# Recurrence gates as two 64-row products at once, one channel tile at a time, with the pooling sums as scans and the mixer's shift on ScalarE

## The chip, the core and the metric

The kernel is one launch on one core of a Trainium2 chip. The metric is the device time of that launch in microseconds (us), as the median of three runs. What can be told from no change is about 0.2%, some 2 us here.

Five engines matter. PE is TensorE: it loads a stationary operand ("LDWEIGHTS", shown as PEld) and streams a moving operand past it ("MATMUL"). DVE is VectorE and ACT is ScalarE; ACT loads a table ("ACT_TABLE_LOAD") when the family of functions changes. POOL is GpSimd, and SP starts transfers. Each engine works through its own queue strictly in order: an instruction that waits holds up everything behind it on that engine. Matrix products land in PSUM, from which DVE or ACT read them.

## The reference: what is computed

One layer of a decoder trunk, for 1024 tokens of width 1024, in fp32. The part that the change touches is the mixer:

```python
proj = rms_norm(h) @ w_in              # 1024 x 1536: u_pool, u_lru, u_gate
# four pooling groups of 128 channels, windows 2, 4, 8, 16
outs.append((c - c_lag) / count - ug)  # mean of the last w tokens, less the token
y_pool = (einsum('bsgc,gcd->bsgd', d, pool_w) + pool_b) * pool_scale
# recurrence: 512 channels in 8 heads of 64
xb = causal_depthwise_conv(u_lru)
r = sigmoid(einsum('bshi,hij->bshj', uh, gate_a_w) + gate_a_b)
i = sigmoid(einsum('bshi,hij->bshj', uh, gate_x_w) + gate_x_b)
a = exp(8 * r * log_sigmoid(lru_L)); b = sqrt(1 - a**2) * (i * xb)
h_t = a_t * h_(t-1) + b_t              # then multiplied by gelu(u_gate)
h = h + concat(y_pool, y_lru) @ w_out
```

Behind it come a squared-ReLU MLP of width 4096, a gated per-layer embedding and a final norm, which the change leaves alone.

## The kernel before, in words

**Tiling.** Everything stands channels by tokens: a tile is 128 channels on the partitions by 1024 tokens. Each fp32 operand x is held as a pair x_hi, x_lo in the matrix engine's fp32r format, and a product is three MATMULs, hi·hi, hi·lo and lo·hi (`mm`, L310 to L328; the instruction is on L320). A MATMUL has a 128 x 128 stationary block and a moving operand of 512 tokens, so one 128-channel block against 1024 tokens is six MATMULs. `split` (L149 to L156) makes a pair: ACT copies the high part (L152), DVE subtracts it to get the low part (L153). Weights come ahead of use through a list, `todo`: fetched as wi_raw, split to wi_hi and wi_lo, two buffers each, so the split of one projection's weights begins when the projection two before it has ended.

**The mixer.** `project(i)` (48 MATMULs into ps_i) makes one 128-channel tile of the input projection. Its order before is: conv of four channel tiles (results H[0] to H[3], split into the pairs B[4] to B[7], which the trace calls y), project(0), project(1), gates of tiles 0 and 1, project(2), project(3), gates of tiles 2 and 3, project(4), the pooling products of groups 0 and 1 (`pool_mix(0)`), project(5), project(6), `pool_mix(1)`, project(7), project(8). `lru_gates(pair)` multiplies a channel tile by two 128 x 128 blocks, for r and i, each holding two heads of 64 x 64 on its diagonal and zeros elsewhere; ACT takes the sigmoids straight from PSUM (L526), and DVE multiplies i by the conv's result (L527). `lru_scan` is Exp, Tanh, Square and Sqrt on ACT (L533 to L541) and a first-order scan on DVE (L544). `pool_windows` sums a window of w tokens by log2(w) shifted adds (L561) with a copy of the head each (L562), then scales and subtracts (L564 to L566) and splits. `pool_mix` multiplies a group by its 128 x 128 weights, and DVE adds the bias and scales (L578).

**What sets the order.** A list scheduler in the framework turns the written order into one queue for each engine, by what is free first; the order is fixed when the program is built. PSUM is handed out by `psum` (L130 to L135) in turns: an odd turn takes one tile of [128, 1024] from a pool of two ("pp", names such as ps_i_931), an even turn takes two tiles of [128, 512] from a pool of four ("pd", names such as ps_i_0_481 and ps_i_512_482). A tile that is asked for waits until the tile that held its place has been read. The projections' results are read by DVE (`normed`, L489), the gates' results by ACT.

```python
    def psum(name, one=False):
        turn.append(name)
        if one or len(turn) % 2 == 1:
            return [(slice(0, S), banks(name))]
        return [(hs, bank(f"{name}_{hs.start}")) for hs in HALVES]
```

Of the kernel before, what the change touches and what calls it, by code (L numbers as in the profile page):

```python
# [9 lines left out]
AF = mybir.ActivationFunctionType  # L10
ALU = mybir.AluOpType

P = 128
S = 1024
D = 1024
DFF = 4096
HALF = 512
# [11 lines left out]
NLRU = 4  # L29
NPOOL = 4  # L30
# [7 lines left out]
COLS = {}  # L38
# [11 lines left out]
def block_kernel(  # L50
# [16 lines left out]
    nc = tc.nc  # L67
# [9 lines left out]
    H = [h_all[:, i] for i in range(NT)]  # L77
# [47 lines left out]
    def hl(i):  # L125
        return small[i // 2][:, HALVES[i % 2]]
# [3 lines left out]
# [6 lines that stand above are left out]
# [4 lines left out]
    def col(name, i):  # L140
        c = COLS[name] + i
        return vecs[:, c : c + 1]
# [161 lines left out]

    def small_weights(name, raw):
        hi, lo = hl(2), hl(3)
        split(raw, hi, lo)
        return hi, lo
# [21 lines left out]
    def kblk(t, k):  # L330
        return t[:, k * P : (k + 1) * P]
# [78 lines left out]
    def tables():  # L410

        one = ones_f[:, :16]
        tc.keep_in_program_order(
            nc.vector.tensor_tensor_scan(recip_t, one, one, 0.0, ALU.mult, ALU.add)
        )
        nc.vector.reciprocal(recip_t, recip_t)


        tc.keep_in_program_order(nc.vector.memset(T[5], 0.0))
        rv = T[5].rearrange("p (n a t c) -> p n a t c", n=2, a=2, t=2)  # L420
        for pair in range(2):
            for a in range(2):
                for par in range(2):
                    r = slice(64 * par, 64 * par + 64)
                    nc.sync.dma_start(rv[r, pair, a, :, r], gates[pair, a, par])

# [34 lines left out]
    lv = vecs[:, c0 : c0 + NLRU]  # L461
    neg, e, s, s2, poly, cpos, cneg = (sp[:, i] for i in range(7))
    nc.vector.tensor_scalar_mul(neg, lv, -1.0)
# [12 lines left out]
    nc.vector.scalar_tensor_tensor(cpos, poly, 16.0, neg, ALU.mult, ALU.add)  # L476
    nc.vector.tensor_scalar_mul(cneg, cpos, -1.0)

    def project(i):
# [24 lines left out]
    LSETS = ((H[4], H[5], H[6]), (H[7], T[3], T[4]))  # L504

    gate_w, mix_w = {}, {}

    def ask_gates(pair):
        gate_w[pair] = small_weights(f"gw{pair}", T[5][:, pair * HALF : (pair + 1) * HALF])

    def ask_mix():
        raw = wp.tile([P, S], F32, tag="raw", name="pw_raw")[:, :HALF]
        nc.sync.dma_start(raw, pool_w)
        mix_w[0] = small_weights("pw", raw)

    def lru_gates(pair):

        hi, lo = gate_w[pair]
        for t in range(2):
            o = 2 * pair + t  # L520
            ct, rt, _ = LSETS[t]
            for a, (dst, b) in enumerate(((rt, "ga_b"), (ct, "gx_b"))):
                ps = psum(f"ps_g{a}{o}")
                mm(ps, kblk(hi, 2 * a + t), kblk(lo, 2 * a + t), *B[4 + o], True, True)
                for hs, part in ps:
                    nc.scalar.activation(dst[:, hs], part, AF.Sigmoid, bias=col(b, o))  # L526
            nc.vector.tensor_tensor(H[o], H[o], ct, ALU.mult)  # L527

# [24 lines left out]
    def pool_windows(g, ps):  # L553
        w = WINDOWS[g]
        u, *st = T[:3]
        if ps:
            normed(u, ps)
        cur, step, n = u, 1, 0
        while step < w:
            nxt = st[n % 2]  # L560
            nc.vector.tensor_tensor(nxt[:, step:], cur[:, step:], cur[:, : S - step], ALU.add)  # L561
            nc.vector.tensor_copy(nxt[:, :step], cur[:, :step])  # L562
            cur, step, n = nxt, 2 * step, n + 1
        nc.vector.tensor_tensor(cur[:, : w - 1], cur[:, : w - 1], recip_t[:, : w - 1], ALU.mult)  # L564
        nc.vector.tensor_tensor(cur[:, : w - 1], cur[:, : w - 1], u[:, : w - 1], ALU.subtract)
        nc.vector.scalar_tensor_tensor(  # L566
            cur[:, w - 1 :], cur[:, w - 1 :], 1.0 / w, u[:, w - 1 :], ALU.mult, ALU.subtract
        )
        split(cur, *B[g])

    def pool_mix(pair):
        whi, wlo = mix_w[0]
        for t in range(2):
            g = 2 * pair + t
            ps = psum(f"ps_p{g}")
            mm(ps, kblk(whi, g), kblk(wlo, g), *B[g], True, True)
            for hs, part in ps:
                nc.vector.tensor_scalar(  # L578
                    T[5][:, hs], part, col("pool_b", g), col("pool_s", g), ALU.add, ALU.mult
                )  # L580
            split(T[5], *B[g])

    conv(0, ps_l[0])
    conv(1, ps_l[1])
    ask_gates(0)
    conv(2, ps_l[2])
    conv(3, project(0))
    pool_windows(0, project(1))
    lru_gates(0)
    ask_gates(1)  # L590
    pool_windows(1, project(2))
    ps = project(3)
    normed(T[0], ps)
    lru_scan(0)
    lru_gates(1)
    ask_mix()
    pool_windows(2, None)
    ps = project(4)
    pool_mix(0)
    pool_windows(3, ps)  # L600
# [513 lines left out]
```

## Time and profile before

| | |
|---|---|
| Median of three runs | 977.63 us (977.19 to 978.01) |
| The profiled execution | 977.54 us, of which the span from first to last instruction is 975.5 us |
| Mean granted TensorE clock | 0.998 |
| PE busy | 964.8 us, 99% of the span |
| DVE busy | 757.0 us, 78% |
| ACT busy | 442.7 us, 45% |
| The mixer's projections, gates and pooling products on PE | from 40.77 us to 155.01 us |

The profile is of one execution; its times are counted from the first instruction. A line L153 is line 153 of the kernel; names are those of the program's tiles with the buffer numbers left out, so `y<-h` on L152 is the high part of one of the pairs B. "[4.06 <-DVE t L489]" behind a row says that the engine stood idle for 4.06 us before it, and that DVE's instruction on L489 ended the wait. Ends of MATMULs are modelled and overlap the next one's start; the distance between starts is what counts. On DVE and ACT, too, a row's duration overlaps the next one's start by about 0.1 us, so a queue's length is counted from start to start.

### The profile page before, as it was taken

Reading aid. Unit: us, or ns where it says so; the run is one execution under the profiler, and the core shown is the slowest. Engines: PE = TensorE matmul, PEld = TensorE weight load, DVE = VectorE, ACT = ScalarE, POOL = GpSimd, SP = SyncE. Lnnn points to the kernel's source line nnn. Section 1 sums busy time; section 2 is a strip of 40 time slices with the busy share of each in tenths; the row PEclk is TensorE's granted clock in tenths of the full one; section 3 lists DMA queues with packets and bytes.
Section 4 is the critical chain, followed back from the end, with each engine's and each line's share of the span. In section 5 each row is a group of like instructions: output and inputs, shape, how many; then the busy total and the mean of one; then the engine's idle time right before and its main releaser. Section 6 shows DMA issues by size and latency. Waiting matters only on the chain.

```text
span 975.5 us, 11507 instructions
## 1 busy us (share of the span) xinstructions
PE 964.8 (99%) x4472; PEld 805.2 (83%) x4472; DVE 757.0 (78%) x885; ACT 442.7 (45%) x528; POOL 99.1 (10%) x72
## 2 busy tenths in 40 slices
PE   9999999999999999999999999999999999999996
PEld 7888888888788888888888888888888888888996
DVE  7999995449887777677777899879775669784976
ACT  7377643336543343334333544444343337552534
POOL 0000000002523322332331000000000000000210
PEclk9999999999999999999999999999999999999999
DMA  6301243110245345434533897356532341031122
GB/s 231 105 23 33 87 151 107 45 43 30 82 152 201 119 140 177 159 119 160 196 119 137 307 368 254 110 194 202 174 118 90 108 151 44 3 127 44 44 87 87
DMA packets 46198, 125.04 MB, mean 128 GB/s; under 512 B 5312, under 2 KB 7360, under 8 KB 46144
## 3 DMA queue, kind: packets, MB, share of 16 engines
q1 hardware_dynamic: 46000, 124.27, 36.9%
q8 instruction: 35, 0.57, 0.2%
q14 instruction: 19, 0.16, 0.1%
q10 hardware_dynamic: 144, 0.04, 0.0%
HBM read 90.74 MB, written 33.55 MB: 127 GB/s over the span
## 4 chain that ended last, share of the span: by engine, by line
PE 95%; DVE 3%; ACT 1%; DMA 1%; issue 0%; SPq 0%; DVEq 0%
PE ps_P_u L320 31%; PE ps_P_d L320 31%; PE ps_i L320 10%; PE ps_o L320 9%; PE ps_e L320 8%; PE ps_l L320 3%; PE ps_g L320 1%; PE ps_j L320 1%; PE ps_p L320 1%; DVE h L968 1%; DMA h<-in_xT 1%; DVE a L153 1%; DVE a L156 0%; DVE t L984 0%; DVE wu_lo L153 0%
## 5 line engine op out<-in xcount | busy, mean ns | idle before, releaser
L320 PE MATMUL ps_P_d<-a,wd_P_hi 128*128 128x512 f32 x880 | 271.1, 389 | 0.0
L320 PEld LDWEIGHTS ps_P_d<-a,wd_P_hi 128*128 128x128 f32 x880 | 165.2, 188 | 34.4
L320 PE MATMUL ps_P_d<-a,wd_P_lo 128*128 128x512 f32 x440 | 171.3, 389 | 0.0
L320 PE MATMUL ps_P_u<-a,wu_hi 128*128 128x512 f32 x512 | 157.7, 389 | 0.0
L320 PE MATMUL ps_P_u<-y,wu_hi 128*128 128x512 f32 x384 | 118.1, 389 | 0.0
L320 PEld LDWEIGHTS ps_P_u<-a,wu_hi 128*128 128x128 f32 x512 | 96.1, 188 | 19.9
L659 DVE TENSOR_TENSOR t<-t,ps_P_u 128x512 f32<-128x512 f32 (+1 forms) x80 | 62.6, 784 | 47.9 <-PE ps_P_u L320 47.7
L320 PE MATMUL ps_P_u<-a,wu_lo 128*128 128x512 f32 x256 | 99.6, 389 | 0.0
L320 PEld LDWEIGHTS ps_P_d<-a,wd_P_lo 128*128 128x128 f32 x440 | 82.6, 188 | 17.4 <-DVE wd_P_lo L153 0.3
L320 PEld LDWEIGHTS ps_P_u<-y,wu_hi 128*128 128x128 f32 x384 | 72.1, 188 | 14.9
L320 PE MATMUL ps_i<-a,wi_hi 128*128 128x512 f32 x288 | 77.1, 389 | 0.0
L320 PE MATMUL ps_P_u<-y,wu_lo 128*128 128x512 f32 x192 | 74.8, 390 | 0.4 <-DVE wu_lo L153 0.4
L153 DVE TENSOR_TENSOR a<-wd,a 128x1024 fp32r<-128x1024 f32 x56 | 67.1, 1219 | 5.2 <-ACT a L152 4.1
L152 ACT ACTIVATE a<-wd 128x1024 fp32r<-128x1024 f32 x56 | 58.8, 1057 | 21.2 <-PE ps_P_d L320 10.2
L320 PE MATMUL ps_o<-y,wo_hi 128*128 128x512 f32 x256 | 68.4, 389 | 0.0
L320 PEld LDWEIGHTS ps_i<-a,wi_hi 128*128 128x128 f32 x288 | 54.1, 188 | 11.2
L152 ACT ACTIVATE wu_hi<-wu 128x1024 fp32r<-128x1024 f32 x24 | 25.5, 1062 | 78.3 <-PE ps_P_u L320 43.9
L152 ACT ACTIVATE wu_hi<-wu_raw 128x1024 fp32r<-128x1024 f32 (+1 forms) x25 | 25.3, 1011 | 78.2 <-PE ps_P_u L320 44.8
L320 PEld LDWEIGHTS ps_P_u<-a,wu_lo 128*128 128x128 f32 x256 | 48.0, 188 | 10.0
L320 PEld LDWEIGHTS ps_o<-y,wo_hi 128*128 128x128 f32 x256 | 48.0, 188 | 10.0
L152 ACT ACTIVATE wd_P_hi<-wd 128x1024 fp32r<-128x1024 f32 x24 | 25.4, 1060 | 58.2 <-PE ps_P_d L320 58.0
L153 POOL TENSOR_TENSOR wg_lo<-wg_raw,wg_hi 128x1024 fp32r<-128x1024 f32 x4 | 9.9, 2478 | 408.7 <-DVE h L953 382.1
(224 smaller groups left out, 1634.2 us busy)
## 6 DMA issues: line engine op xcount, KB each, us to landing
wd<-act SPq DMA_DIRECT2D x56, 512.0 KB, 5.6
act<-t SPq DMA_DIRECT2D x32, 512.0 KB, 4.3
wu_raw<-in_w_up SPq DMA_DIRECT2D x16, 512.0 KB, 3.7
wu<-in_w_up SPq DMA_DIRECT2D x16, 512.0 KB, 4.6
act<-wu SPq DMA_DIRECT2D x16, 512.0 KB, 4.5
wd<-in_w_down SPq DMA_DIRECT2D x16, 512.0 KB, 6.2
h<-in_xT SPq DMA_DIRECT2D x15, 512.0 KB, 4.3
wg_raw<-in_w_gate SPq DMA_DIRECT2D x12, 512.0 KB, 3.3
```

Source lines behind the costliest of these rows:

```text
L152: pin(nc.scalar.activation(hi, src, AF.Copy))
L153: pin((eng or nc.vector).tensor_tensor(lo, src, f32(hi), ALU.subtract))
L320: ins = nc.tensor.matmul(ps, w, z[:, hs], start=first and z is zhi and w is whi, stop=last and w is wlo, skip_group_check=more,)
L659: (eng or nc.vector).tensor_tensor(to, to if y is None else y, x, ALU.add)
L968: nc.vector.scalar_tensor_tensor(hv, hv, col("g_fin", o), rfin[:, hs], ALU.mult, ALU.mult)
```

## The change

**Gates.** The zero blocks go. For each channel tile, head 0 (channels 0 to 63) and head 1 (channels 64 to 127) each get a stationary block of 64 rows by 128 columns, that head's r and i weights side by side. The two heads are issued in turn, one on the upper 64 rows of the array and one on the lower 64, into two PSUM results, each of which holds r for one head and i for the same head on its two halves of partitions. So there are as many gate MATMULs as before, 48, each on 64 rows. The sigmoids are taken by halves of the partitions: six ACT instructions on 64 partitions for each channel tile in place of three on 128. The gates' weights come in one transfer of 256 KB, with neither the clearing of T[5] nor the eight smaller transfers, and are split once, into the slots hl(0) and hl(1); the mixer's weights take hl(2) and hl(3).

**Order.** `lru_gates` is called for one channel tile at a time: behind project(0), project(1), project(3) and project(4).

**Pooling.** For the windows 4, 8 and 16 the sums are a scan over the first w tokens and a scan over the rest that adds the token that enters and subtracts the one that leaves, in place of two, three and four adds with their copies. The window of 2 stays.

**Shift.** The mixer's bias and scale are one ACT instruction for each part (Identity with scale and the bias pool_bs = pool_b · pool_scale), in place of DVE's.

```diff
@@ -302,8 +302,8 @@
-    def small_weights(name, raw):
-        hi, lo = hl(2), hl(3)
+    def small_weights(raw, i):
+        hi, lo = hl(i), hl(i + 1)
         split(raw, hi, lo)
         return hi, lo
...
@@ -416,13 +416,7 @@
-        tc.keep_in_program_order(nc.vector.memset(T[5], 0.0))
-        rv = T[5].rearrange("p (n a t c) -> p n a t c", n=2, a=2, t=2)
-        for pair in range(2):
-            for a in range(2):
-                for par in range(2):
-                    r = slice(64 * par, 64 * par + 64)
-                    nc.sync.dma_start(rv[r, pair, a, :, r], gates[pair, a, par])
+        nc.sync.dma_start(T[5][:, FIRST], gates)
...
@@ -476,6 +470,9 @@
+    c_b, c_s = COLS["pool_b"], COLS["pool_s"]
+    nc.vector.tensor_tensor(pool_bs, vecs[:, c_b : c_b + NPOOL], vecs[:, c_s : c_s + NPOOL], ALU.mult)
+
...
@@ -503,28 +500,39 @@
+    HEADS = slice(0, 64), slice(64, P)
     gate_w, mix_w = {}, {}
 
-    def ask_gates(pair):
-        gate_w[pair] = small_weights(f"gw{pair}", T[5][:, pair * HALF : (pair + 1) * HALF])
+    def ask_gates():
+        gate_w[0] = small_weights(T[5][:, FIRST], 0)
 
     def ask_mix():
         raw = wp.tile([P, S], F32, tag="raw", name="pw_raw")[:, :HALF]
         nc.sync.dma_start(raw, pool_w)
-        mix_w[0] = small_weights("pw", raw)
-
-    def lru_gates(pair):
-
-        hi, lo = gate_w[pair]
-        for t in range(2):
-            o = 2 * pair + t
-            ct, rt, _ = LSETS[t]
-            for a, (dst, b) in enumerate(((rt, "ga_b"), (ct, "gx_b"))):
-                ps = psum(f"ps_g{a}{o}")
-                mm(ps, kblk(hi, 2 * a + t), kblk(lo, 2 * a + t), *B[4 + o], True, True)
-                for hs, part in ps:
-                    nc.scalar.activation(dst[:, hs], part, AF.Sigmoid, bias=col(b, o))
-            nc.vector.tensor_tensor(H[o], H[o], ct, ALU.mult)
+        mix_w[0] = small_weights(raw, 2)
+
+    def lru_gates(o):
+
+
+        hi, lo = gate_w[0]
+        ct, rt, _ = LSETS[o % 2]
+        zhi, zlo = B[4 + o]
+        ps = [psum(f"ps_g{h}{o}") for h in range(2)]
+        halves = [
+            [(hs.start + n, x[:, n : n + HALF]) for hs, x in parts for n in range(0, hs.stop - hs.start, HALF)]
+            for parts in ps
+        ]
+        for n, (w, z) in enumerate(((hi, zhi), (hi, zlo), (lo, zhi))):
+            for (at, x0), (_, x1) in zip(*halves):
+                for r, x in zip(HEADS, (x0, x1)):
+                    nc.tensor.matmul(
+                        x, w[r, o * P : (o + 1) * P], z[r, at : at + HALF], start=n == 0, stop=n == 2
+                    )
+        for dst, b, rows in ((rt, "ga_b", HEADS), (ct, "gx_b", HEADS[::-1])):
+            for h, r in enumerate(rows):
+                for hs, part in ps[h]:
+                    nc.scalar.activation(dst[HEADS[h], hs], part[r], AF.Sigmoid, bias=col(b, o)[r])
+        nc.vector.tensor_tensor(H[o], H[o], ct, ALU.mult)
 
     def lru_scan(pair):
         for t in range(2):
@@ -555,12 +563,16 @@
         u, *st = T[:3]
         if ps:
             normed(u, ps)
-        cur, step, n = u, 1, 0
-        while step < w:
-            nxt = st[n % 2]
-            nc.vector.tensor_tensor(nxt[:, step:], cur[:, step:], cur[:, : S - step], ALU.add)
-            nc.vector.tensor_copy(nxt[:, :step], cur[:, :step])
-            cur, step, n = nxt, 2 * step, n + 1
+        cur = st[g % 2]
+        if w == 2:
+            nc.vector.tensor_tensor(cur[:, 1:], u[:, 1:], u[:, : S - 1], ALU.add)
+            nc.vector.tensor_copy(cur[:, :1], u[:, :1])
+        else:
+
+            nc.vector.tensor_tensor_scan(cur[:, :w], ones_f[:, :w], u[:, :w], 0.0, ALU.mult, ALU.add)
+            nc.vector.tensor_tensor_scan(
+                cur[:, w:], u[:, w:], u[:, : S - w], cur[:, w - 1 : w], ALU.add, ALU.subtract
+            )
         nc.vector.tensor_tensor(cur[:, : w - 1], cur[:, : w - 1], recip_t[:, : w - 1], ALU.mult)
         nc.vector.tensor_tensor(cur[:, : w - 1], cur[:, : w - 1], u[:, : w - 1], ALU.subtract)
         nc.vector.scalar_tensor_tensor(
@@ -575,27 +587,28 @@
             ps = psum(f"ps_p{g}")
             mm(ps, kblk(whi, g), kblk(wlo, g), *B[g], True, True)
             for hs, part in ps:
-                nc.vector.tensor_scalar(
-                    T[5][:, hs], part, col("pool_b", g), col("pool_s", g), ALU.add, ALU.mult
+                nc.scalar.activation(
+                    T[5][:, hs], part, AF.Identity, bias=pool_bs[:, g : g + 1], scale=col("pool_s", g)
                 )
             split(T[5], *B[g])
 
     conv(0, ps_l[0])
     conv(1, ps_l[1])
-    ask_gates(0)
+    ask_gates()
     conv(2, ps_l[2])
     conv(3, project(0))
+    lru_gates(0)
     pool_windows(0, project(1))
-    lru_gates(0)
-    ask_gates(1)
+    lru_gates(1)
     pool_windows(1, project(2))
     ps = project(3)
     normed(T[0], ps)
     lru_scan(0)
-    lru_gates(1)
+    lru_gates(2)
     ask_mix()
     pool_windows(2, None)
     ps = project(4)
+    lru_gates(3)
     pool_mix(0)
     pool_windows(3, ps)
     gate_out(0, project(5))
@@ -1069,17 +1082,20 @@
...
+    gx_b = np.roll(cols(gate_x_b), 64, axis=0)
...
-    gates = np.stack([np.asarray(g)[0].reshape(2, 2, 2, 64, 64) for g in (gate_a_w, gate_x_w)])
-    gates = gates.transpose(1, 0, 3, 4, 2, 5)
+    ga, gx = (np.asarray(g)[0].reshape(NLRU, 2, 64, 64) for g in (gate_a_w, gate_x_w))
+    gates = np.stack([np.stack([ga[:, 0], gx[:, 0]], 2), np.stack([gx[:, 1], ga[:, 1]], 2)])
+    gates = gates.transpose(0, 2, 1, 3, 4)
```

Three places in the queues. The first is PE behind project(0), whose last MATMULs write ps_i_0 and ps_i_512. y_121 and y_122 are the pair B[4] that channel tile 0's gates read; before, project(1) follows at once:

```order
L320 MATMUL ps_i_0_488<-a,wi_hi 128x512
L320 MATMUL ps_i_512_489<-a,wi_hi 128x512
L320 MATMUL ps_i_0_488<-a,wi_lo 128x512
L320 MATMUL ps_i_512_489<-a,wi_lo 128x512
L320 MATMUL ps_i_552<-a,wi_hi 128x512 x4
L320 MATMUL ps_i_552<-a,wi_lo 128x512 x2
```

And in the changed program:

```order
L320 MATMUL ps_i_0_481<-a,wi_lo 128x512
L320 MATMUL ps_i_512_482<-a,wi_lo 128x512
L528 MATMUL ps_g_539<-y_121,hl_135 128x512
L528 MATMUL ps_g_0_540<-y_121,hl_135 128x512
L528 MATMUL ps_g_539<-y_121,hl_135 128x512
L528 MATMUL ps_g_512_541<-y_121,hl_135 128x512
L320 MATMUL ps_i_567<-a,wi_hi 128x512 x3
L528 MATMUL ps_g_539<-y_122,hl_135 128x512
L528 MATMUL ps_g_0_540<-y_122,hl_135 128x512
```

The twelve gate MATMULs of tile 0 now stand between project(0) and project(1), with three of project(1)'s (ps_i_567) between the first four and the last eight.

The second place is ACT around the window of 8, whose result is split as y_117. Before, all gates' sigmoids (L526) are over by then:

```order
L526 ACTIVATE t<-ps_g_512_808,vecs 128x512
L526 ACTIVATE h<-ps_g_817,vecs 128x1024
L152 ACTIVATE hl_136<-pw_raw 128x512
L533 ACT_TABLE_LOAD
L533 ACTIVATE h<-h,sp 128x1024
L533 ACTIVATE h<-t,sp 128x1024
L534 ACTIVATE h<-h,sp 128x1024
L535 ACTIVATE h<-h 128x1024
L152 ACTIVATE y_117<-t 128x1024
```

And in the changed program, where L534 is the sigmoid and L541 to L543 are Exp, Tanh and Square:

```order
L152 ACTIVATE y_117<-t 128x1024
L541 ACT_TABLE_LOAD
L541 ACTIVATE h<-h,sp 128x1024
L542 ACTIVATE h<-h,sp 128x1024
L543 ACTIVATE h<-h 128x1024
L152 ACTIVATE wi_hi<-wi_raw 128x1024
L534 ACT_TABLE_LOAD
L534 ACTIVATE t<-ps_g_0_873,vecs 64x512
L534 ACTIVATE t<-ps_g_872,vecs 64x1024
L534 ACTIVATE t<-ps_g_512_874,vecs 64x512
L534 ACTIVATE h<-ps_g_872,vecs 64x1024
```

The sigmoids of channel tile 3 (ps_g_872, 873, 874) now stand behind the split y_117. ps_g_872 is a "pp" tile; by the turns, the next two "pp" tiles are those of pooling group 0 and of project(5), so project(5) takes the place of ps_g_872 and begins no sooner than the last row above has read it. Before, project(5) took the place of ps_g_817, which the second row of the fence before had read.

The third place is DVE up to the window of 8's result. Before (L561 is an add, L562 a copy, L565 the last step, L527 the gates' product):

```order
L561 TENSOR_TENSOR t<-t 128x1023
L562 COPY t<-t 128x1
L153 TENSOR_TENSOR wi_lo<-wi_raw,wi_hi 128x1024
L527 TENSOR_TENSOR h<-h 128x1024
L561 TENSOR_TENSOR t<-t 128x1022
L527 TENSOR_TENSOR h<-h 128x1024
L153 TENSOR_TENSOR hl_136<-pw_raw,hl_136 128x512
L562 COPY t<-t 128x2
L561 TENSOR_TENSOR t<-t 128x1020
L562 COPY t<-t 128x4
L566 SCALAR_TENSOR_TENSOR t<-t 128x1017
L564 TENSOR_TENSOR t<-t,recip_t 128x7
```

And in the changed program (L572 and L573 are the two scans, L552 the recurrence's scan, L535 the gates' product):

```order
L572 SCALAR_TENSOR_TENSOR t<-ones,t 128x8
L153 TENSOR_TENSOR wi_lo<-wi_raw,wi_hi 128x1024
L552 SCALAR_TENSOR_TENSOR h<-h,t 128x1024
L573 SCALAR_TENSOR_TENSOR t<-t 128x1016
L576 TENSOR_TENSOR t<-t,recip_t 128x7
L578 SCALAR_TENSOR_TENSOR t<-t 128x1017
L577 TENSOR_TENSOR t<-t 128x7
L535 TENSOR_TENSOR h<-h 128x1024
```

Three adds and three copies became two scans, and both gate products that stood ahead of the window's result now stand behind it.

More of the change, by code (lines that the diff above doesn't have):

```diff
@@ L461, in block_kernel @@
     lv = vecs[:, c0 : c0 + NLRU]
-    neg, e, s, s2, poly, cpos, cneg = (sp[:, i] for i in range(7))
+    neg, e, s, s2, poly, cpos, cneg, pool_bs = (sp[:, i] for i in range(8))
     nc.vector.tensor_scalar_mul(neg, lv, -1.0)
@@ L1074 @@
             cols(norm_mix_g), cols(norm_mlp_g), cols(norm_ple_g), cols(norm_final_g), cols(pool_b),
-            cols(pool_scale), conv, cols(conv_b), cols(gate_a_b), cols(gate_x_b), cols(lru_L),
+            cols(pool_scale), conv, cols(conv_b), cols(gate_a_b), gx_b, cols(lru_L),
             cols(b_ple_gate),
@@ L1093 @@
         "pool_w": c(np.asarray(pool_w)[0].transpose(1, 0, 2)).reshape(P, NPOOL * P),
-        "gates": c(gates),
+        "gates": c(gates).reshape(P, NLRU * P),
         "w_out": tiles(np.asarray(w_out)[0]),
```

## The prediction

> **What bounds the kernel now.** First the page's busy times and its chain of waits, to see which engine sets the end:
>
> ```profile
> PE 964.8 (99%) x4472; PEld 805.2 (83%) x4472; DVE 757.0 (78%) x885; ACT 442.7 (45%) x528; POOL 99.1 (10%) x72
> PE 95%; DVE 3%; ACT 1%; DMA 1%; issue 0%; SPq 0%; DVEq 0%
> ```
>
> PE is busy for 99% of the span, so a microsecond that PE stands idle in the mixer is a microsecond on the end, and one taken out of PE's work is gained, if PE has nothing else to wait for. The chain through the mixer (start, length, group) shows what is there to gain:
>
> ```profile
> 40.77 21.76 PE ps_i L320 x96
> 62.53 4.08 PE ps_g L320 x18
> ...
> 66.83 1.36 PE ps_g L320 x6
> ...
> 89.73 5.44 PE ps_g L320 x24
> ...
> 108.77 21.76 PE ps_i L320 x96
> ```
>
> The pieces follow each other without a gap: 21.76 / 96 = 0.227 us for each MATMUL of 512 tokens, and 48 gate MATMULs are 10.88 us. The view of waits, PE's own, gives its longest:
>
> ```profile
> PE ps_l L432 <- DVE ones L338: 1.3, 1, 1.3
> PE n_ps L394 <- DVE t L1037: 0.6, 1, 0.6
> ```
>
> Neither is in the mixer. So a gain must come from the gate MATMULs, and a loss from a wait that isn't there now. Then I followed DVE's and ACT's queues in the timeline, since both are nearly full (DVE 7.50 of 7.50 us, then 17.81 of 19.00; ACT 7.47, then 14.44):
>
> ```profile
> 62.50:70.00 7.50, 7.50 (x35) 6.21 (x34) 7.50 (x9) 7.47 (x10) 0.00 (x0) 1.00 0.19 70
> 70.00:89.00 19.00, 19.00 (x86) 15.73 (x85) 17.81 (x24) 14.44 (x14) 0.00 (x0) 1.00 0.13 42
> ```
>
> **The gate products.** If the two heads' MATMULs run beside each other, a pair takes what one takes now, and 24 x 0.227 = 5.44 us leave PE's queue. The trace has no 64-row MATMUL. Its bounds: no overlap, gain 0; full overlap, 5.44 us. I take the second, because the queue can feed one load and MATMUL each 0.114 us (2.74 us for 24, from start to start):
>
> ```profile
> 949.22 2.90 PE L320 MATMUL ps_e<-a 128*128 128x256 f32 x24
> 951.96 0.87 PE L320 MATMUL ps_j<-proj,proj 128*128 128x256 f32 x6
> ```
>
> The order changes ten times between 64 and 128 rows. Each change costs between 0 and 0.35 us (a MATMUL of 389 ns and a load of 188 in sequence, less the 227 of a step); I take 0, as the sum hardly depends on it (below). The Trainium skill, "TensorEngine Tiling (Array Packing)", Key Properties, says that a change of tiling mode drains the engine; no run so far shows that, and by it the ten changes would take up to 3.5 us of the 5.44.
>
> **Tile 0's gates come early.** They stand right behind project(0). In ACT's timeline:
>
> ```profile
> 51.28 1.06 ACT L152 ACTIVATE wi_hi<-wi_raw 128x1024 fp32r<-128x1024 f32 x1 [5.01 <-issue]
> 52.24 2.00 ACT L152 ACTIVATE y<-h 128x1024 fp32r<-128x1024 f32 x2
> ...
> 62.11 1.06 ACT L152 ACTIVATE wi_hi<-wi_raw 128x1024 fp32r<-128x1024 f32 x1 [0.36 <-PE ps_i L320]
> ```
>
> The wi_hi split at 51.28 waits for the end of project(0), and the first y stands behind it: its first half ends at about 53.25. PE, done with project(0) at 51.65 (40.77 + 10.88), waits some 1.6 us for y_121. DVE's y_122 comes 1.2 later (a subtraction like the adds below), and seven MATMULs ahead of it cover 1.1 of that. So project(1) ends at 51.65 + 1.8 + 1.4 (six pairs) + 10.9, about 65.7, where it was 62.5.
>
> **ACT late, DVE late.** ACT's next wi_hi waits for that end. From there its queue, with starts from these rows:
>
> ```profile
> 91.69 2.27 ACT L526 ACTIVATE h<-ps_g,vecs 128x512 f32<-128x512 f32 x3
> 93.84 1.28 ACT L526 ACTIVATE t<-ps_g,vecs 128x512 f32<-128x512 f32 x2
> 95.25 1.12 ACT L526 ACTIVATE h<-ps_g,vecs 128x1024 f32<-128x1024 f32 x1
> 100.67 1.16 ACT L533 ACTIVATE h<-t,sp 128x1024 f32<-128x1024 f32 x1 [1.11 <-DVE h L527]
> 101.73 1.13 ACT L534 ACTIVATE h<-h,sp 128x1024 f32<-128x1024 f32 x1
> 104.14 1.06 ACT L152 ACTIVATE y<-t 128x1024 fp32r<-128x1024 f32 x1 [0.32 <-DVE t L565]
> 105.10 1.14 ACT L534 ACTIVATE t<-t,sp 128x1024 f32<-128x1024 f32 x1
> 106.14 1.05 ACT L535 ACTIVATE t<-h 128x1024 f32<-128x1024 f32 x1
> 107.20 1.28 ACT L541 ACT_TABLE_LOAD   x1
> 108.50 1.06 ACT L541 ACTIVATE h<-h 128x1024 f32<-128x1024 f32 x1
> ```
>
> Start to start: a split 0.96, a table 1.30, Exp 1.06, Tanh 1.04, Square 1.06, a sigmoid of 1024 tokens 1.02, of 512 0.57 ((2.15 - 1.02) / 2). I give 64 partitions the time of 128, for the row counts tokens; half of it would be the lower bound. Wi_hi, table, Exp, y, table, three sigmoids, y_113, three sigmoids, Tanh and Square are 13.0 us: 65.7 becomes 78.7. Square frees DVE's L545 (L537 before). Before, that instruction stood ahead of DVE's restart at 78.66; now it is that restart.
>
> **The window of 8 on DVE.** Before, its result is there at 103.94 + 0.17 = 104.11:
>
> ```profile
> 78.66 1.29 DVE L489 TENSOR_TENSOR t<-ps_i,rstd 128x512 f32<-128x512 f32 x2 [1.19 <-PE ps_i L320]
> 92.64 2.28 DVE L544 TENSOR_TENSOR_SCAN h<-h,t 128x1024 f32<-128x1024 f32 x1
> 94.83 1.20 DVE L561 TENSOR_TENSOR t<-t 128x1023 f32<-128x1023 f32 x1
> 95.95 0.14 DVE L562 COPY t<-t 128x1 f32<-128x1 f32 x1
> 97.14 1.22 DVE L527 TENSOR_TENSOR h<-h 128x1024 f32<-128x1024 f32 x1
> 98.28 1.22 DVE L561 TENSOR_TENSOR t<-t 128x1022 f32<-128x1022 f32 x1
> 103.94 0.17 DVE L565 TENSOR_TENSOR t<-t 128x7 f32<-128x7 f32 x1
> ```
>
> From 78.7 on the queue loses five adds (1.13 each, 5.65), five copies (0.54) and both L527 (1.14 each, 2.28), and gains two long scans (2.20, as the recurrence's scan), two short ones (0.1) and L545 (1.14): 104.11 - 8.47 + 5.74 = 101.4. Bounds for a long scan: 1.13 as the adds, 2.20 as L544; I take 2.20, the same instruction on the same engine. The window of 16 behind it changes nothing for PE.
>
> **The new wait.** project(5)'s result goes to the place of ps_g_872, whose last sigmoid stands on ACT behind y_117, and y_117 waits for 101.4. From there: split 0.96, table 1.30, Exp 1.06, Tanh 1.04, Square 1.06, wi_hi 0.96, table 1.30, sigmoids 0.57, 1.02, 0.57 and the fourth to its end 1.12: 10.96 us, so project(5) starts at 112.4, where it started at 108.77: **+3.6 us**. PE would get there at 108.77 - 5.44 + 1.8 = 105.1 (up to 1 us later, for DVE reads ps_i4 behind y_118), so it stands idle for about 6 us, and the 5.44 us gained go into that. That is why overlap and mode changes hardly count. They enter only through project(1)'s end: without overlap 1.4 us later.
>
> Behind the wait, ACT has 5.7 us of shifts more and DVE that much less:
>
> ```profile
> L578 DVE TENSOR_SCALAR t<-ps_p,vecs x6: 798/802/1334, 109.0 to 142.5; 128x512 f32<-128x512 f32 x4, 128x1024 f32<-128x1024 f32 x2
> 109.00:133.00 24.00, 24.00 (x107) 19.87 (x107) 23.97 (x29) 8.94 (x9) 0.00 (x0) 1.00 0.23 81
> ```
>
> ACT has 15 of 24 us free there and DVE none, so this costs nothing and eases DVE; without that room it would be 5.7 us. The one transfer for eight and the memset lie before 40 us, beside PE's first products: 0.
>
> **The clock after the wait.** PE's only longer rest is the program's start, and there MATMULs come slowly:
>
> ```profile
> 1.31 4.64 PE L432 MATMUL ps_l<-ones 128*128 128x512 f32 x10 [1.31 <-DVE ones L338]
> 5.74 0.83 PE L320 MATMUL ps_l<-a,wl_hi 128*128 128x512 f32 x2
> ```
>
> Ten take 4.43 us, 0.443 each, where 2.27 would do: 2.2 us lost (the page's clock row doesn't show it). No wait of 6 us inside the program is in the trace. Bounds 0 and 2.2; I take 2.2, the start being the only rest of such length. The Trainium skill, "TensorE: Matmul & The Clock Gate", Part 1, has the array at half rate after an idle window of about 3.4 us until it has been busy for as long; the start agrees (4.43 us), and by its figure I estimate 1.7 us.
>
> **Sum.** 977.54 + 3.6 + 2.2 = 983.3 us; the profiled execution is 0.1 below the median, which I leave out.
>
> **Rivals.**
> (a) The wait without the slow clock: 977.5 + 3.6 = 981.1. For it: the clock row never shows a drop. Against: the start.
> (b) The gain arrives. If ACT reaches ps_g_872's fourth sigmoid before PE needs the place at 105.1, PE alone decides: 977.5 - 5.4 + 1.8, 973.9, and up to 3.5 more with mode changes. This asks for a result of the window of 8 at 94.5, 7 us sooner than worked out. Scans at the adds' rate give 2.1 of it, sigmoids at half their time another 2 to 4; all must come together.
> (c) Both cancel in part: scans at the adds' rate alone put project(5) at 110.3, so 979.1, or 981.3 with the slow clock; with sigmoids faster too, about 977.5.
> (d) Pairs that don't overlap: project(1) ends 1.4 us later, and with mode changes 0.5 more; 984.7 to 985.2.
>
> **How the numbers follow.** Forecast (wait and slow clock) 0.52; (a) 0.24; (b) 0.07; (c) 0.09; (d) 0.08. The likeliest one's own range is 982 to 984.6. The range for all, 978.8 to 985.2, leaves out (b) and parts of (c) and (d). A measurement of this kernel tells 0.2%, about 2 us, from no change: below 975.7 is faster, 0.06; between, 0.10 (the rest of (b), most of (c)); slower 0.84.
>
> **What would show it.** In the changed profile: a PE wait of about 2 us ahead of the first ps_g, on ACT's y; ps_g MATMULs in pairs 0.23 us apart; the L573 scans at 2.2 us; y_117 at about 101.4 and ACT's sigmoids of 64x512 at 0.69; a PE wait of about 6 us ahead of a ps_i, on ACT's L534, with that ps_i at 112.4; the ten or so MATMULs behind it 0.44 us apart; from there on all as before, later by 5.8. The forecast is wrong if PE's wait there is under 2 us, if it is on another engine, or if the end moves by something behind 115 us.

## The result, and the profile after

The changed kernel takes **985.34 us** (median of four runs, 984.95 to 986.67), the kernel before 977.78 us beside it: a ratio of 1.0081, 95% interval 1.0063 to 1.0098. It is slower by 7.6 us. The forecast was 983.3 us with a range up to 985.2: the sign and the mechanism came as told, the size was 2 us too small, and the time lies just outside the range. The term that failed is the +3.6 us by which project(5) was to start late; it measured 5.78 us. The profiled execution took 984.95 us, with a span of 983.2 us.

PE's waits in the changed kernel (engine and line, what it waited for, total, times, longest):

```profile
PE ps_i L320 <- ACT h L534: 6.6, 1, 6.6
PE ps_g L528 <- ACT y L152: 1.7, 1, 1.7
```

Neither stood in the profile of before, and both were forecast: the second is tile 0's gates behind project(0), the first is project(5), which waits for a sigmoid. PE's timeline around them:

```profile
102.83 1.66 PE L528 MATMUL ps_g<-y,hl 64*128 64x512 f32 x12
104.42 3.53 PE L320 MATMUL ps_p<-y,hl 128*128 128x512 f32 x12
114.55 2.07 PE L320 MATMUL ps_i<-a,wi_hi 128*128 128x512 f32 x4 [6.60 <-ACT h L534]
...
117.28 1.75 PE L320 MATMUL ps_i<-a,wi_hi 128*128 128x512 f32 x4
```

Tile 3's gates and the pooling products of groups 0 and 1 (ps_p) end at 107.95; then PE rests until 114.55. The first six MATMULs behind the rest take 2.73 us from start to start (114.55 to 117.28), where six times 0.227 are 1.36. The view of windows has the granted clock in the column ahead of the last two (102 to 114.5 us, then 114.5 to 119):

```profile
102.00:114.50 12.50, 5.85 (x28) 3.54 (x27) 9.48 (x13) 11.41 (x11) 0.00 (x0) 0.90 0.12 42
114.50:119.00 4.50, 4.45 (x11) 3.53 (x12) 3.20 (x3) 4.43 (x6) 0.00 (x0) 0.53 0.35 120
```

The chain of waits gives both parts their size. Before, project(5) and project(6) started at 108.77 and their 96 MATMULs took 21.76 us:

```profile
113.39 1.12 ACT h L534
114.55 23.96 PE ps_i L320 x96
...
163.00 17.23 PE ps_o L320 x76
```

The start is 5.78 us later, the 96 MATMULs take 2.20 us more, and from there on every piece has its old length: the output projection starts at 163.00 instead of 155.01. That is the whole loss: 7.99 us there, 7.7 us in the spans (983.2 and 975.5).

### The profile page after: what moved, and what is told of

Same layout as the page of the kernel before. It is cut to its first block, busy times and chain, and to the rows that moved or that the text cites. A ratio compares the mean times of both kernels' runs of the same rounds, so it can differ in the third digit from the quotient of the medians.

```text
span 983.2 us, 11513 instructions
## 1 busy us (share of the span) xinstructions
PE 964.2 (98%) x4472; PEld 801.4 (82%) x4472; DVE 747.3 (76%) x866; ACT 465.2 (47%) x551; POOL 99.1 (10%) x72
## 4 chain that ended last, share of the span: by engine, by line
PE 89%; DVE 5%; ACT 3%; issue 2%; DMA 1%; SPq 0%; DVEq 0%
PE ps_P_d L320 31%; PE ps_P_u L320 30%; PE ps_o L320 9%; PE ps_e L320 8%; PE ps_i L320 6%; PE ps_l L320 3%; PE ps_j L320 1%; DMA h<-in_xT 1%; DVE h L981 1%; ACT t L534 0%; DVE h L552 0%; ACT y L152 0%; DVE wu_lo L153 0%; ACT h L534 0%; DVE a L153 0%
## 5 line engine op out<-in xcount | busy, mean ns | idle before, releaser
L320 PE MATMUL ps_i<-a,wi_hi 128*128 128x512 f32 x288 | 79.3, 397 | 6.6 <-ACT h L534 6.6
```

The costliest lines, as they stand in the source:

```text
L320: ins = nc.tensor.matmul(ps, w, z[:, hs], start=first and z is zhi and w is whi, stop=last and w is wlo, skip_group_check=more,)
```

## The experiments

Each is an edit to the changed kernel, unless it says otherwise. The starts of all pieces shift by up to a microsecond from one execution to the next (project(0) starts at 40.8 us before, at 39.7 in the first run below), so distances are compared, not starts alone.

### The order on ACT alone

```diff
+                    sig = nc.scalar.activation(dst[HEADS[h], hs], part[r], AF.Sigmoid, bias=col(b, o)[r])
...
+        return sig.ins        # lru_gates: tile's last sigmoid
...
-    lru_gates(3)
+    last = lru_gates(3)
...
-    lru_scan(1)
+    with tc.issue_after(last):
+        lru_scan(1)
```

> The changed kernel with one order added: ACT's Exp, Tanh, Square and Sqrt of lru_scan(1) stand behind the last sigmoid of channel tile 3. Theory (project(5) waits for ps_g_872 because these stand ahead of its sigmoids): the sigmoids follow y_117's split at about 104.0 with no table load between, the fourth ends at about 108.1, PE is through with the pooling products at 107.95, so project(5) starts at about 108.2 instead of 114.55, and with no rest there is no slow clock either: 985.3 - 6.3 - 2.2 = 976.8 us (976 to 978). Rival (another wait, on DVE's reading of ps_i4 or on the pooling results, would hold PE anyway): 981 or more, with a PE wait on DVE of over 3 us.

Measured: 976.92 us, ratio to before 1.0002 (0.9993 to 1.0011). ACT's timeline, and PE's behind it:

```profile
101.82 1.06 ACT L152 ACTIVATE y<-t 128x1024 fp32r<-128x1024 f32 x1 [5.66 <-DVE t L578]
102.79 1.04 ACT L152 ACTIVATE wi_hi<-wi_raw 128x1024 fp32r<-128x1024 f32 x1
103.86 2.53 ACT L534 ACTIVATE t<-ps_g,vecs 64x512 f32<-64x512 f32 x3
106.41 2.39 ACT L534 ACTIVATE h<-ps_g,vecs 64x1024 f32<-64x1024 f32 x3
```

```profile
107.57 1.20 PE L320 MATMUL ps_i<-a,wi_hi 128*128 128x512 f32 x4 [0.77 <-ACT h L534]
```

Exp, Tanh, Square and two table loads no longer stand between y_117 (the first row) and the sigmoids, and DVE's part of the scan stands later with them; but for table loads the work is the same. The wait falls from 6.60 to 0.77 us, the slow clock is gone, and so is the whole loss. The cause is the place that project(5) gets in PSUM together with ACT's order. It is no gain over before yet: what the gates save goes into the wait of 1.69 us for y_121, these 0.77 us, and a gap of some 0.5 us between the two pooling products (their twelve MATMULs take 3.54 us with the border ahead of them, 2.88 before).

### The rest and the slow clock

```diff
-            mm(ps, kblk(whi, g), kblk(wlo, g), *B[g], True, True)
+            for _ in range(5 if g == 1 else 1):
+                mm(ps, kblk(whi, g), kblk(wlo, g), *B[g], True, True)
```

> The changed kernel with the second pooling product of pool_mix(0) computed five times over into the same PSUM tile: 24 MATMULs more, 5.4 us, in the place where PE rested for 6.6 us. Theory (the slow MATMULs behind the wait come from the rest): project(5) still starts at about 114.5, the rest before it is about 1.2 us, its MATMULs are 0.227 us apart from the first on, and 985.3 becomes 983.1 us (982.6 to 983.7). Rival (they are slow for another reason, the change of product or the reading of PSUM by ACT): still 0.44 us apart, 985.3 us.

Measured: 983.34 us, ratio 1.0067 (1.0052 to 1.0082), with PE's rows

```profile
103.85 9.01 PE L320 MATMUL ps_p<-y,hl 128*128 128x512 f32 x36
114.02 1.20 PE L320 MATMUL ps_i<-a,wi_hi 128*128 128x512 f32 x4 [1.16 <-ACT h L534]
```

24 MATMULs more, and the kernel is no slower: 6.5 us above its before, where the changed kernel was 7.6 above (the intervals of the two ratios overlap). The rows say more. Project(5) starts as late as ever (73.7 us behind project(0) in both), but its first four MATMULs take 1.20 us instead of 2.07, and by the chain its and project(6)'s 96 take 22.08 instead of 23.96. So the slow MATMULs come from the rest; filling it gets 1.9 of their 2.2 us back in the profiled execution. The other 0.3 us are there at a full clock too: the late scan above has 22.05 for the same 96, behind its 0.77 us.

### 128-row gates in the new places

```diff
+    def lru_gates(o):      # before's products and sigmoids, one tile at a time
+        pair, t = divmod(o, 2)
+        hi, lo = gate_w[pair]
...
+        for a, (dst, b) in enumerate(((rt, "ga_b"), (ct, "gx_b"))):
+            ps = psum(f"ps_g{a}{o}")
+            mm(ps, kblk(hi, 2 * a + t), kblk(lo, 2 * a + t), *B[4 + o], True, True)
```

> The changed kernel with the gate products as before (128 x 128 blocks with zeros, three sigmoids on 128 partitions a tile), in the new places, with the new pooling and the shift on ACT. Theory (the places make the wait, the halved sigmoids lengthen it): PE's gate work is back to 10.9 us, so it reaches project(5) at about 110.5; ACT is shorter by three sigmoids a tile; project(5) starts at about 112, after a rest of 1 to 2 us that is too short for the slow clock: 977.7 + 3.3 = 981.0 us (980 to 982.5). Rival (the 64-row form itself costs the time): 977 to 978 us.

Measured: 980.34 us, ratio 1.0039 (1.0024 to 1.0053); project(5) starts at 112.00 behind this wait:

```profile
PE ps_i L320 <- ACT t L527: 1.3, 1, 1.3
```

So 3.5 of the 7.6 us are lost without any 64-row product: this part belongs to the places. Project(5) starts 71.3 us behind project(0); in the changed kernel it was 73.7, before 68.0. What the 64-row form adds is on ACT: here project(5)'s place is free behind one sigmoid on 128 partitions (110.83 to 111.94), there behind the fourth on 64 (110.88 to 114.51). And as PE comes later and the place is free sooner, the rest is short and the clock stays full.

### Tile 3's gates beside tile 2's

```diff
     lru_gates(2)
+    lru_gates(3)
     ask_mix()
     pool_windows(2, None)
     ps = project(4)
-    lru_gates(3)
```

> The changed kernel with the gates of tile 3 right behind those of tile 2, both behind project(3) as before the change. Theory: project(5) no longer finds tile 3's gates in its place, so the wait of 6.6 us and the slow clock go; in exchange tile 3's products wait up to 3 us for PSUM, which DVE (project(3)'s result) and ACT (tile 2's sigmoids) must first read. 978.7 us (977.5 to 980.5). Rival (the wait only moves in full): 983 or more.

Measured: 980.33 us, ratio 1.0041 (1.0026 to 1.0056), 1.6 us above what was expected. Project(5) no longer waits; the wait for PSUM has moved to tile 3's gates, as told, and 2.85 us of it were enough to slow the clock, which I hadn't reckoned with:

```profile
94.42 1.65 PE L528 MATMUL ps_g<-y,hl 64*128 64x512 f32 x11 [2.85 <-DVE t L486]
```

```profile
96.00:104.00 8.00, 8.00 (x29) 6.46 (x29) 8.00 (x8) 7.04 (x9) 0.00 (x0) 0.79 0.19 66
96.07 12.70 PE ps_i L320 x48
```

Project(4) takes 12.70 us (the second line is from the chain), in the changed kernel 11.10 from the end of tile 2's gates to tile 3's (91.73 to 102.83): 1.6 us, the whole of what was not expected.

### The pooling products moved

```diff
     lru_gates(3)
-    pool_mix(0)
     pool_windows(3, ps)
     gate_out(0, project(5))
     lru_scan(1)
+    pool_mix(0)
     gate_out(1, project(6))
-    pool_mix(1)
     gate_out(2, project(7))
+    pool_mix(1)
     gate_out(3, project(8))
```

> The changed kernel with the pooling products moved only: groups 0 and 1 behind project(5), groups 2 and 3 behind project(7). By the turns of PSUM project(5) then takes the place of channel tile 2's gates, whose sigmoids ended at 97.3. Theory (the loss is the place that project(5) gets, and the rest and the slow clock that follow): the wait of 6.6 us and the slow clock go, PE's wait of 1.7 us for y_121 stays, and four times twelve gate MATMULs in about 1.6 us save 10.9 - 6.5 = 4.4 us: 977.6 + 1.7 - 4.4 = 974.9 us (974 to 976.5). Rival (the wait moves to the pooling products, which now take tile 3's place): 979 us or more.

Measured: 976.60 us, ratio 0.9993 (0.9983 to 1.0002). The large wait is gone and none has taken its place. But 1.7 us of the expected gain are missing. In the profiled execution, where nothing at all is gained (the output projection starts 114.27 us behind project(0), before 114.24), 1.4 us of it are to be seen: behind the wait for y_121, which is as long as in the changed kernel, the clock was low this time.

```profile
52.66 0.73 PE L528 MATMUL ps_g<-y,hl 64*128 64x512 f32 x4 [1.69 <-ACT y L152]
53.32 0.99 PE L320 MATMUL ps_i<-a,wi_hi 128*128 128x512 f32 x3
54.24 2.08 PE L528 MATMUL ps_g<-y,hl 64*128 64x512 f32 x8
```

```profile
53.00:58.00 5.00, 5.00 (x20) 3.13 (x17) 5.00 (x5) 4.92 (x6) 0.00 (x0) 0.66 0.02 3
```

The changed kernel's row for the same stretch, behind the same wait of 1.69 us, has the clock at 1.00:

```profile
53.00:58.00 5.00, 4.57 (x23) 3.03 (x24) 5.00 (x6) 4.94 (x6) 0.00 (x0) 1.00 0.01 3
```

From the first gate MATMUL of tile 0 to that of tile 1 it took 14.6 us here (52.66 to 67.25) and 13.1 there (53.43 to 66.57). The rest of the shortfall is in the gates, whose twelve MATMULs cost more than the 1.6 us of the expectation (next experiment). Whether the slow clock also holds the median back is not shown: five of the ten executions have a mean granted clock of 0.995 or 0.996, the other five of 0.997 or 0.998, and the times of the first, 976.15 to 976.77 us, lie among those of the second, 975.05 to 977.16. In the late scan's ten executions the three with 0.996 did take longer, 978.04 to 978.63 us against at most 977.20.

### Tile 0's gates inside project(1)

As the one before, and

```diff
-    lru_gates(0)
-    pool_windows(0, project(1))
+    pre = gate_ps(0)       # PSUM in the same turns as before
+    pool_windows(0, project(1, lambda: lru_gates(0, pre), 0))   # behind its first step
```

> As e5_mix_later, and channel tile 0's gates are written behind the first of the eight steps of project(1) instead of ahead of it, with PSUM given out in the same turns. Theory: the wait of 1.7 us for y_121 is covered by project(1)'s MATMULs, and project(1) ends earlier by it, so ACT and DVE behind it too: 974.9 - 1.7 = 973.2 us (972.5 to 974.5). Rival (tile 0's sigmoids come later and hold project(2)'s place in PSUM): 975 us or more.

Measured: **973.63 us**, ratio to before 0.9965 (0.9952 to 0.9977): faster than both kernels, by 3.6 and some 11 us. PE has no wait left in the mixer, and the chain shows what the 64-row products give:

```profile
40.58 12.69 PE ps_i L320 x56
...
64.84 1.59 PE ps_g L533 x12
66.43 21.98 PE ps_i L320 x96
...
89.99 11.11 PE ps_i L320 x48
101.10 1.59 PE ps_g L533 x12
```

Twelve gate MATMULs take 1.59 us instead of 2.72, and each stretch of projections between them 0.22 us more than its 21.76 or 10.88. So a tile costs 1.59 + 0.22 = 1.81 us. Full overlap alone would be 1.36 us for a tile; the other 0.45 stand at the borders between 64 and 128 rows, 0.22 for each of the two. Tile 0's gates cost more, because three MATMULs of project(1) divide them: from project(0)'s start to tile 1's gates it takes 24.26 us, 2.50 more than the 21.76 of the 96 projections. Together the four tiles cost 7.93 us and save 10.88 - 7.93 = 2.95, and that is what the profiles show: the output projection starts 111.30 us behind project(0) here (40.58 to 151.88), before 114.24. That the medians differ by 3.6 us (2.2 to 4.7 by the interval of the ratio) and not by 2.95 is within what the starts shift.

### One head behind the other

As the one before, and

```diff
-        for n, (w, z) in enumerate(((hi, zhi), (hi, zlo), (lo, zhi))):
-            for (at, x0), (_, x1) in zip(*halves):
-                for r, x in zip(HEADS, (x0, x1)):
+        for h, r in enumerate(HEADS):
+            for n, (w, z) in enumerate(((hi, zhi), (hi, zlo), (lo, zhi))):
+                for at, x in halves[h]:
```

> As e6_gates0_inside, with all six MATMULs of one head ahead of the six of the other, so that neighbours are on the same 64 rows. Theory (the gain is that two MATMULs on different rows run at once): twelve take about 2.7 us instead of 1.6, and the time is 973.2 + 4.4 = 977.6 us (976.5 to 978). Rival (a MATMUL of 64 rows is short by itself): 973.2 us.

Measured: 975.70 us, ratio 0.9984 (0.9975 to 0.9993), between the two expectations. Twelve MATMULs take

```profile
64.96 2.16 PE ps_g L533 x12
```

2.16 us, 0.57 more than in pairs, in tiles 1 to 3. Tile 0's, which stand in two parts, take no longer than before (2.97 us from the first of them to project(1)'s next, 53.27 to 56.24; in pairs 2.96, 53.20 to 56.16). Three times 0.57 is 1.7 us, and by the chain the output projection starts 113.06 us behind project(0) instead of 111.30. So putting the heads in turn is worth some 1.7 of the 2.95 us. But 2.16 is below the 2.72 of one after the other, so some of the second head's MATMULs still ran beside the first's. The single rows of the trace tell which: the first two start alone (64.89 and 65.23), then four pairs start at 65.46, 65.69, 65.93 and 66.15, the second of each 0.01 to 0.12 us behind the first, and the last two again alone (66.51 and 66.73). That is eight steps instead of six or twelve: the second head's first MATMUL (its row has 0.49 us, as the very first of the twelve; the others have 0.38 or 0.39) started with the first head's third, though by the edit three more of that head stand ahead of it.

### A shorter rest

The fill of the second experiment, with four products in place of five.

> As e2_fill with 18 MATMULs more instead of 24, so that PE rests some 2.5 us ahead of project(5). e4_gates23 had a slow clock behind a rest of 2.85 us, e2_fill none behind 1.2, e3_full_rows none behind 1.3. If a rest of 2.5 us by itself is enough for the slow clock: project(5)'s first MATMULs 0.44 us apart and about 985.3 us. If it isn't: 0.227 us apart and 983.3 us.

One execution: 983.65 us. By its time it would be no slow clock, but project(0) started 0.7 us earlier than in the changed kernel, and the rows are plain:

```profile
113.89 1.84 PE L320 MATMUL ps_i<-a,wi_hi 128*128 128x512 f32 x4 [2.50 <-ACT h L534]
113.89 23.64 PE ps_i L320 x96
112.00:116.00 4.00, 2.11 (x6) 1.67 (x7) 3.64 (x6) 3.92 (x6) 0.00 (x0) 0.77 0.50 174
```

(from the timeline, the chain and the windows). Counted from project(0), the output projection starts at 121.8 us, in the changed kernel at 122.1, with the longer fill at 120.3. A rest of 2.50 us is enough for the slow clock; the 96 MATMULs take 23.64 us, 1.6 more than the 22.08 behind the rest of 1.16 us.

### The old pooling and the old shift

The fastest version above, with the shifted adds and with the mixer's shift on DVE, as before the change.

> As e6_gates0_inside, with the pooling sums as shifted adds and the mixer's shift on DVE, as before the change; so only the 64-row gate products, their places and those of the pooling products are new. Theory (PE alone sets the end in e6_gates0_inside, the new pooling and the shift lie beside it): 973.6 us (973 to 974.5). Rival (DVE, which gets 5.7 us of shifts and some 3 us of adds back, holds PE somewhere): 975.5 us or more.

Measured: 973.84 us, ratio 0.9974 (0.9965 to 0.9984), beside 973.63 (the intervals of the ratios overlap). By the chain the output projection starts 111.30 us behind project(0) in both. The scans and the shift on ACT, the two other parts of the change, do nothing for the time in that version that these runs can tell; the gain is that of the gate products, in places where PE doesn't wait.

### What the sigmoids' steps depend on

In the changed kernel a sigmoid of 512 tokens follows another after 0.58 us or after 0.70. Two orders of the six sigmoids of a tile; the first is shown, the second has the loop over h, the half that is written, outermost:

```diff
-        for dst, b, rows in ((rt, "ga_b", HEADS), (ct, "gx_b", HEADS[::-1])):
-            for h, r in enumerate(rows):
+        for r in HEADS:                        # by the half that is read
+            for dst, b, rows in ((rt, "ga_b", HEADS), (ct, "gx_b", HEADS[::-1])):
+                h = rows.index(r)
```

> The changed kernel with each tile's six sigmoids in another order: first those that read partitions 0 to 63 of PSUM, then those that read 64 to 127. In the changed kernel's trace a sigmoid follows the one before it by its duration less 0.11 us where both read and write the same half, and by its whole duration where the half changes. If the half that is read decides: steps of 0.58 and 1.02 us between sigmoids of different results that read the same half. If the half that is written decides: 0.70 and 1.14 there. No statement on the time.

> The counterpart of e10_by_input_half: first the sigmoids of the first PSUM result, which read 0 to 63 and then 64 to 127 and write partitions 0 to 63, then those of the second. If the half that is written decides: steps of 0.58 and 1.02 us within the three sigmoids' six that write the same half, also where the half that is read changes. If the half that is read decides: 0.70 and 1.14 there. No statement on the time.

Times of one execution each: 985.81 and 985.54 us, as the changed kernel. Tile 1's last sigmoids by the half that is read, then by the half that is written:

```profile
76.10 1.12 ACT L535 ACTIVATE t<-ps_g,vecs 64x1024 f32<-64x1024 f32 x1
77.23 1.26 ACT L535 ACTIVATE h<-ps_g,vecs 64x512 f32<-64x512 f32 x2
78.51 1.16 ACT L543 ACTIVATE h<-h,sp 128x1024 f32<-128x1024 f32 x1
```

```profile
76.62 1.11 ACT L535 ACTIVATE t<-ps_g,vecs 64x1024 f32<-64x1024 f32 x1
77.75 1.11 ACT L535 ACTIVATE h<-ps_g,vecs 64x1024 f32<-64x1024 f32 x1
```

In the first, both rows read partitions 64 to 127 and the written half changes between t and h: the step is 1.13 us, the whole duration. In the second both write 64 to 127 and the read half changes: 1.13 again. The two of 512 in the first, which read and write the same halves, take 1.26 together, 0.10 less than two durations of 0.68. So neither theory holds alone: either change costs the overlap of 0.11 us. The change of the result (ps_g) and of the destination (t to h) is not the reason: before, on 128 partitions, three sigmoids of 512, 512 and 1024 tokens whose durations add up to 2.49 us take 2.15 up to the next result's first (91.69 to 93.84), so that step has its overlap too.

## Why the prediction was right and where it was wrong

**What bounds the kernel**: right. The new wait of PE in the mixer and the slow MATMULs behind it went to the end: 7.99 us at the start of the output projection, 7.7 in the spans.

**The gate products**: right that neighbours overlap and that it hardly counts here; the mode changes are not 0 but 0.22 us each, inside the bounds of 0 and 0.35. In the changed kernel they count only through project(1)'s end. The Trainium skill, "TensorEngine Tiling (Array Packing)", Key Properties, says that a change of mode drains the engine. The traces fit that: twelve MATMULs and their two borders take 1.81 us where 1.36 would do.

**Tile 0's gates come early**: right, 1.69 us of wait against 1.6. Project(1) ended later than told, the next product starting at 66.57 instead of 65.7: tile 0's gates stand in two parts, and their four borders are 0.9 us. But ACT's split of the next wi_hi starts somewhat ahead of that end, at 66.23, as it did before (62.11, the next product at 62.37); the prediction put it at the end itself. So 0.5 us of the 0.9 reached ACT.

**ACT late, DVE late**: the mechanism right, the sum too small. This is the first step that failed, a term that was sized too small: the 13.0 us of ACT's queue became 13.8. ACT from project(1)'s end to Square:

```profile
66.23 1.06 ACT L152 ACTIVATE wi_hi<-wi_raw 128x1024 fp32r<-128x1024 f32 x1 [1.66 <-PE ps_i L320]
67.31 1.28 ACT L541 ACT_TABLE_LOAD   x1
...
72.02 2.39 ACT L534 ACTIVATE t<-ps_g,vecs 64x512 f32<-64x512 f32 x3
74.44 1.06 ACT L152 ACTIVATE y<-t 128x1024 fp32r<-128x1024 f32 x1
75.52 2.38 ACT L534 ACTIVATE h<-ps_g,vecs 64x512 f32<-64x512 f32 x3
77.93 1.15 ACT L542 ACTIVATE h<-h,sp 128x1024 f32<-128x1024 f32 x1
78.99 1.04 ACT L543 ACTIVATE h<-h 128x1024 f32<-128x1024 f32 x1
```

I took every ACT instruction at its step in the trace of before. Three sigmoids were 2.16 us by that; they take 2.42, because a change of halves costs the overlap. A split was 0.96; where a table load or a sigmoid stands behind it, it takes 1.08 (66.23 to 67.31, 74.44 to 75.52). The taken rows were of splits with a like instruction behind them.

**The window of 8 on DVE**: right. From its restart to the result 22.9 us against 22.7; the long scans take 2.31 us, the short ones 0.17. Only the restart came at 80.06 instead of 78.7:

```profile
80.06 1.22 DVE L545 SCALAR_TENSOR_TENSOR h<-h 128x1024 f32<-128x1024 f32 x1 [0.90 <-ACT h L543]
99.29 2.31 DVE L573 TENSOR_TENSOR_SCAN t<-t 128x1016 f32<-128x1016 f32 x1
102.77 0.16 DVE L577 TENSOR_TENSOR t<-t 128x7 f32<-128x7 f32 x1
```

**The new wait**: right in its place and its releaser. This is the second step that failed, for the same reason: ACT's queue from y_117 to the fourth sigmoid was put at 10.96 us and took 11.55. That the wait's length, 6.60 us, is near the "about 6" of the prediction is luck: its own figures, 105.1 and 112.4, give 7.3. Both were too early, project(5) by 2.15 us and PE's arrival (107.95) by 1.9 to 2.9, for the borders of the gates were taken as 0 and the gap between the pooling products was not in it.

```profile
102.96 1.06 ACT L152 ACTIVATE y<-t 128x1024 fp32r<-128x1024 f32 x1 [5.66 <-DVE t L577]
104.04 1.28 ACT L541 ACT_TABLE_LOAD   x1
105.34 1.15 ACT L541 ACTIVATE h<-h,sp 128x1024 f32<-128x1024 f32 x1
106.52 1.15 ACT L542 ACTIVATE h<-h,sp 128x1024 f32<-128x1024 f32 x1
107.58 1.04 ACT L543 ACTIVATE h<-h 128x1024 f32<-128x1024 f32 x1
108.53 1.04 ACT L152 ACTIVATE wi_hi<-wi_raw 128x1024 fp32r<-128x1024 f32 x1
109.58 1.28 ACT L534 ACT_TABLE_LOAD   x1
110.88 2.50 ACT L534 ACTIVATE t<-ps_g,vecs 64x512 f32<-64x512 f32 x3
113.39 2.39 ACT L534 ACTIVATE h<-ps_g,vecs 64x1024 f32<-64x1024 f32 x3
```

The terms of the miss: the start of the wi_hi split 0.5, ACT to Square 0.85, DVE 0.15, ACT to the fourth sigmoid 0.6, together 2.1 us. So project(5) starts at 114.55 instead of 112.4, and +3.6 became +5.8.

**The shift on ACT**: right, nothing in PE's chain behind 114.55 changed its length.

**The clock after the wait**: right in its kind, and shown by the fill, which gets 1.9 of the 2.20 us back. That the size is so near the 2.2 is partly luck: 0.3 us come with any rest, also at a full clock, and by the view of windows the clock is at 0.50 from 111.9 to 118.7 us, of which 2.7 us fall on the rest itself.

**The rivals**: (a), (b) and (c) asked for a sooner sigmoid or a full clock, and neither came. (d), pairs that don't overlap, gave about the measured time for a reason that the trace refutes. The range was too narrow at its upper end: it took in a later project(1), but no bound for ACT's steps, though the whole sum stood on some twenty of them.

## What to carry to other kernels

Where an engine's queue of short instructions is on the path, take each step from a row that has the same neighbour behind it; 0.1 us here and there in some twenty steps made 1.45 of the 2.1 us of the miss. Before work is moved to be early, see whose buffer its result takes and what stands ahead of its reader: here the gain of some 3 us was real, and the turn of two PSUM tiles turned it into a loss of 7.6 until other products were moved out of that turn. And in these runs a wait of PE cost its length and some 2 us more once it was long enough to lower the clock; MATMULs with no use, put into the wait, got most of that back.

## What the runs showed of the hardware that was not expected

**The clock falls after shorter rests than reckoned.** Rests of 0.8, 1.2 and 1.3 us left it full; 2.50, 2.85 and 6.60 us lowered it, at a cost of 1.6 to 1.9 us beyond the 0.3 that a rest costs at a full clock; and behind tile 0's wait of 1.7 us it stayed at 1.00 in six of the nine profiled executions that have that wait, and fell to 0.66 over the next 5 us in three (the moved pooling products, where it cost 1.4 us, and the two orders of the sigmoids). In narrower windows the low clock is 0.50 throughout and lasts 3.4 us behind the shorter rests (114.2 to 117.6 with the shorter fill, 96.2 to 99.5 with tile 3's gates beside tile 2's), 6.8 us in the changed kernel. Its start doesn't go by the end of the rest: it came 0.3 us behind that end in the first of these, 1.8 us behind it in the second, and 2.7 us ahead of it in the changed kernel. The Trainium skill, "TensorE: Matmul & The Clock Gate", Part 1, puts the bound at idle windows of about 3.4 us; here 2.5 us were enough, and the measurement decides. The windows are free-running by that page, which would fit a rest of one length going either way; what decides between the two behind the 1.7 us no run here shows.

**Half-width instructions on ACT cost more than half.** A sigmoid on 64 partitions takes as long as on 128 (0.68 us for 512 tokens against 0.69, 1.11 for 1024 against 1.12), and where the half read or the half written changes, the next one starts 0.11 us later than it would.

**MATMULs on different 64 rows overlap even when not issued in turn**: 2.16 us for twelve with one head behind the other, against 1.59 in pairs and 2.72 for twelve on 128 rows. The second head's first started with the third in the queue, ahead of its turn.
